# A mixer's u and v as one product in seven parts, with the order of its first half changed

## The chip, the core and the metric

The kernel runs on one core of one Trainium2 chip. The metric is the device time of one execution in microseconds (us), the median over several runs. A profile of one execution gives what each engine did: PE (matmuls), DVE, ACT and POOL (elementwise work), and SP, which like POOL issues transfers.

## The reference

A trunk of two layers over 512 tokens of 1024 channels, in float32. Each layer is a gated feed-forward block, a mixer, and a second feed-forward block; the change is in the mixer.

```python
def rms_norm(x, g):
    y = xf * lax.rsqrt(jnp.mean(xf * xf, axis=-1, keepdims=True) + RMS_EPS)
    return y * g

def mixer(h, w_in, gate_bias, rpb, w_na_out, w_f_out, w_o):    # h = rms_norm(x, gain)
    z = h @ w_in
    q, k, v, uf = four slices of z, 512 columns each;  ga, gf = the rest, 1024 columns each
    y_na = neighbourhood_attention(q, k, v, rpb) @ w_na_out    # 8 heads of 64 channels
    y_f = fourier_mix(uf) @ w_f_out     # real 2-D DFT over positions and 128 channels, 4 groups
    g_na = jax.nn.sigmoid(ga + gate_bias[0])
    g_f = jax.nn.sigmoid(gf + gate_bias[1])
    return (g_na * y_na + g_f * y_f) @ w_o

for l in range(2):
    x = x + 0.5 * swiglu(rms_norm(x, ..), ..)
    x = x + mixer(rms_norm(x, ..), ..)
    x = x + 0.5 * swiglu(rms_norm(x, ..), ..)
return rms_norm(x, final_norm)
```

## The kernel before

Every float32 operand is kept as two parts of a reduced type: a high part, made on ACT (`xh`, `whi`), and the rest, made on DVE (`xl`, `wlo`). A product of two operands is three matmuls, high x high, high x low and low x high (`mm3`, L286 to L288). A 128x512 result fills one of the eight PSUM banks.

**Weights.** `Stream` (object `ws`) walks one list of weight granules of 128x1024, written out by `stage_items` in the order of use. It loads each by a DMA into a `raw` buffer some `FETCH` granules ahead; `prep` then makes `whi` (L175) and `wlo` (L178) from it, with three buffers of each. Sums of weight blocks are made by a second, accumulating DMA on POOL's queue (L146, L180) or on DVE (L160).

**Products in seven parts.** The feed-forward blocks and the mixer's gate and output projections multiply in seven products in place of eight (Strassen's scheme on 2x2 blocks): `strassen` lists the weight blocks a to d and their sums in an order given by product numbers 1 to 7; `product` (L447, L448, L450) runs the 24 matmuls of one product; `snap` (L517) copies an intermediate sum from PSUM, and `less` (L522) subtracts one from PSUM. The mixer's u and v are not made so: `proj_U` makes u, and again u with the token order mirrored, `proj_V` makes v, 96 matmuls of 128x512 each, straight from `xh` and `xl`.

**The norm.** An object made by the stage before holds the transposed input in quads (two channel halves x two token halves). `quad` transposes a quad on PE and splits it, `squares` sums squares on ACT, `rstd` makes the reciprocal root `r` on DVE by three Newton steps, and `spread` (L438, L440) writes `r` to memory and reads it back as the row `R` on all partitions, two DMAs on POOL's queue. For a mixer, `quad` splits straight from PSUM and keeps no raw copy.

**The mixer's order.** Each engine works in order through one queue; the order is mostly as written, with a scheduler that may move work of DVE and ACT by its own due times, except inside `tc.manual_schedule`, where it is as written. The written order of the first half:

- `proj_U`, `proj_V`, `constants()` (tables, by POOL's queue, L951, L954)
- first Fourier stage, `four_pos` for four groups (L1048 to L1051 on DVE)
- projections q0 and k0 (`proj_T`, 24 matmuls; multiplied by R at L970, then split at L292 to L296)
- second Fourier stage, `four_ch` for four groups. Each takes two banks and is evicted by ACT (`fq`) and DVE (`fy`, L1065 to L1067), then split to `y` (L1071, L1072)
- projection q1, then for hp = 0, 1, 2: `att_next(hp)`, projection k of hp+1, the outs of hp-1, projection q of hp+2; then the last steps with rows of y times `w_f_out` (`f_some`) between

`att_next(hp)` is trans(hp-1), 16 transposes of the probabilities (L1140, split to `p` by L292 and L293), then scores(hp), 24 matmuls (L1104); its softmax runs on DVE (L1118, L1127) and ACT (L1124, L1131). `att_outs(hp)`, outs(hp) below, multiplies `p` with v. From step hp = 1 the code reads:

```python
for hp in range(3):
    att_next(hp)
    bias_for(hp + 1)
    proj_k(hp + 1)
    if hp:
        att_outs(hp - 1)
    if hp < 2:
        proj_q(hp + 2)
f_some(2)
```

## Time and profile before

| | |
|---|---|
| Median of three runs | 1904.96 us (1904.66 to 1905.70) |
| Profiled execution | 1906.04 us, of which the span in the profile is 1904.2 |
| PE busy | 1891.7 us, 99% of the span, 9189 matmuls and transposes |
| DVE busy | 1602.4 us, 84% |
| ACT busy | 1161.6 us, 61% |
| POOL busy | 160.7 us, 8% |
| First layer's mixer begins | 337 us |
| Second layer's mixer begins | 1281 us |

A row of the timeline has the start in us, the length in us, engine, line, operation, tiles, size and count, and in brackets how long the engine was idle before it and what ended that. Matmuls are pipelined: a row is longer than the distance to the next, and that distance, the pitch, is what a matmul costs. A line "PE x <- ACT y: a, n, b" of the waits says that PE waited a us in n times, b at the longest, for ACT.

### The profile page before, as it was taken

The numbers are of one execution on the slowest core, as the hardware profiler recorded it, in microseconds if no ns is written. First come the engines' busy times: TensorE is split into PE (matmuls) and PEld (weight loads), VectorE is DVE, ScalarE is ACT, GpSimd is POOL, SyncE is SP. The second block draws the span as 40 slices with busy tenths as digits, with TensorE's granted clock in tenths as the row PEclk, the third lists the DMA queues.
The fourth block names the chain that finished last, engine by engine and source line by source line (L and its number), as shares of the span: only waits on it lengthen the run. The fifth ranks groups of instructions, "written<-read, shape, count | busy, mean of one in ns | idle before, by whom it ended". The sixth has DMA issues, their size and how long they took to land.

```text
span 1904.2 us, 25091 instructions
## 1 busy us (share of the span) xinstructions
PE 1891.7 (99%) x9189; PEld 1586.8 (83%) x9189; DVE 1602.4 (84%) x2000; ACT 1161.6 (61%) x1676; POOL 160.7 (8%) x198
## 2 busy tenths in 40 slices
PE   9999999999999999999999999999999999999998
PEld 7888888888888888888888888888888888888886
DVE  7877899586889987889997778995769899787899
ACT  6655665468566755566665556663675576555655
POOL 0101010000111010001010100100001101000010
PEclk9999999999999999999999999999999999999999
DMA  8776499323886776649877664992247867766594
GB/s 301 202 207 187 150 249 320 105 84 104 217 218 166 180 195 204 177 152 262 251 185 210 187 180 152 268 339 74 68 130 215 215 170 175 207 177 177 170 275 147
DMA packets 104636, 364.36 MB, mean 191 GB/s; under 512 B 12032, under 2 KB 12160, under 8 KB 104512
## 3 DMA queue, kind: packets, MB, share of 16 engines
q1 hardware_dynamic: 77568, 270.70, 40.1%
q0 software_dynamic: 26800, 92.04, 26.8%
q8 instruction: 72, 1.18, 0.2%
q14 instruction: 52, 0.43, 0.1%
q10 hardware_dynamic: 144, 0.02, 0.0%
HBM read 357.46 MB, written 2.11 MB: 189 GB/s over the span
## 4 chain that ended last, share of the span: by engine, by line
PE 95%; issue 2%; DMA 2%; DVE 1%; ACT 0%; POOL 0%; DVEq 0%; ACTq 0%; POOLq 0%; SPq 0%
PE A L447 9%; PE A L448 9%; PE A L450 9%; PE o L448 7%; PE o L447 7%; PE o L450 7%; PE ps L286 5%; PE ps L288 5%; PE ps L287 5%; PE B L448 4%; PE B L447 4%; PE B L450 4%; PE C L448 2%; PE C L447 2%; PE C L450 2%; PE tr L540 2%
## 5 line engine op out<-in xcount | busy, mean ns | idle before, releaser
L175 ACT ACTIVATE whi<-raw 128x1024 fp32r<-128x1024 f32 (+1 forms) x528 | 546.1, 1037 | 423.4 <-PE A L448 123.2
L178 DVE TENSOR_TENSOR wlo<-raw,whi 128x1024 fp32r<-128x1024 f32 (+1 forms) x528 | 627.3, 1193 | 191.2 <-ACT whi L175 186.5
L146 POOL DMA_DIRECT2D raw<-in_wst_dram x158 | 136.2, 873 | 1440.2 <-DMA raw<-in_wst_dram 674.7
L160 DVE TENSOR_TENSOR raw<-raw,raw 128x1024 f32<-128x1024 f32 (+1 forms) x146 | 172.6, 1191 | 1.2
L448 PE MATMUL A<-whi,xl 128*128 128x512 f32 x384 | 149.5, 389 | 0.0
L447 PE MATMUL A<-whi,xh 128*128 128x512 f32 x384 | 149.4, 389 | 0.0
L450 PE MATMUL A<-wlo,xh 128*128 128x512 f32 x384 | 110.5, 389 | 0.0
L170 ACT ACTIVATE whi<-raw 128x1024 fp32r<-128x1024 f32 (+1 forms) x79 | 81.6, 1036 | 40.2 <-PE A L448 12.4
L171 DVE SCALAR_TENSOR_TENSOR wlo<-raw,whi 128x1024 fp32r<-128x1024 f32 (+1 forms) x79 | 93.1, 1193 | 12.2 <-ACT whi L170 12.2
L633 ACT ACTIVATE th<-sn,rh 128x512 f32<-128x512 f32 x80 | 56.8, 714 | 69.4 <-DVE sn L522 69.4
L517 ACT ACTIVATE sn<-A 128x512 f32<-128x512 f32 x96 | 56.4, 589 | 51.3 <-PE A L450 51.2
L450 PEld LDWEIGHTS A<-wlo,xh 128*128 128x128 f32 x384 | 72.1, 188 | 15.0
L448 PEld LDWEIGHTS A<-whi,xl 128*128 128x128 f32 x384 | 72.1, 188 | 14.8
L447 PEld LDWEIGHTS A<-whi,xh 128*128 128x128 f32 x384 | 72.1, 188 | 14.8
L447 PE MATMUL B<-whi,t1h 128*128 128x512 f32 x192 | 76.2, 397 | 0.0
L447 PE MATMUL A<-whi,t3h 128*128 128x512 f32 x192 | 75.3, 392 | 0.4 <-ACT sn L517 0.4
L447 PE MATMUL C<-whi,xh 128*128 128x512 f32 x192 | 74.9, 390 | 0.0
L447 PE MATMUL A<-whi,t2h 128*128 128x512 f32 x192 | 74.9, 390 | 0.0
L448 PE MATMUL B<-whi,t1l 128*128 128x512 f32 x192 | 74.8, 390 | 0.0
L448 PE MATMUL A<-whi,t3l 128*128 128x512 f32 x192 | 74.8, 390 | 0.0
L448 PE MATMUL C<-whi,xl 128*128 128x512 f32 x192 | 74.7, 389 | 0.0
L448 PE MATMUL A<-whi,t2l 128*128 128x512 f32 x192 | 74.7, 389 | 0.0
(409 smaller groups left out, 4748.2 us busy)
## 6 DMA issues: line engine op xcount, KB each, us to landing
raw<-in_wst_dram SPq DMA_DIRECT2D x466, 512.0 KB, 5.4
raw<-in_wst_dram POOLq DMA_DIRECT2D x162, 512.0 KB, 7.9
raw<-in_wst_dram SPq DMA_DIRECT2D x30, 256.0 KB, 3.9
bm<-in_bias_dram SPq DMA_DIRECT2D x16, 384.0 KB, 6.0
vs<-v SPq DMA_DIRECT2D x12, 256.0 KB, 4.9
x<-in_xin_dram SPq DMA_DIRECT2D x4, 512.0 KB, 10.2
raw<-in_wst_dram POOLq DMA_DIRECT2D x8, 256.0 KB, 8.7
dft<-in_dft_dram POOLq DMA_DIRECT2D x8, 256.0 KB, 6.2
```

The costliest lines, as they stand in the source:

```text
L146: G.dma_start(out=self.t, in_=wst[GRAN_AT[self.plus]][:, 0 : self.n], accum_op=ALU.add)
L160: V.tensor_tensor(self.raw.t, self.raw.t, self.add.t, ALU.add)
L170: S.activation(hi, t, AF.Copy, scale=-1.0)
L171: self.last = V.scalar_tensor_tensor(lo, t, -1.0, hi.bitcast(F32), ALU.mult, ALU.subtract)
L175: S.activation(hi[:, cs], t[:, cs], AF.Copy)
L178: self.last = V.tensor_tensor(lo[:, cs], t[:, cs], hi[:, cs].bitcast(F32), ALU.subtract)
L286: PE.matmul(ps, lh, rh, start=start, stop=False, skip_group_check=again)
L287: PE.matmul(ps, lh, rl, start=False, stop=False, skip_group_check=again)
L288: PE.matmul(ps, ll, rh, start=False, stop=stop, skip_group_check=again)
L447: PE.matmul(ps, lh, rh, start=start, stop=False, skip_group_check=again)
L448: PE.matmul(ps, ll, rh, start=False, stop=False, skip_group_check=again)
L450: PE.matmul(ps, lh, rl, start=False, stop=stop, skip_group_check=again)
```

## The change

u and v become one product [u | v] in seven parts (`proj_UV`), in the order 1, 5, 6, 2, 3, 7, 4. u is complete behind the sixth (number 7); its mirrored form is then made from u itself by four matmuls with the mirror matrix. q0, k0, q1 and k1 stand between the products, and the order of DVE and ACT in `proj_UV` is written by hand. The sums of activations need raw quads, so `quad` keeps them for the mixer also; `rstd_steps` takes a square root on ACT and one Newton step; a table load for it stands at the head of the out-projection before a mixer, and one for Exp in the mixer's head. Weight granules of u and v go from 8 to 14 a layer, with loads 8 ahead. The tables are fetched behind product 7, `R` behind product 1.

Behind it the order is: `four_pos`, q2, scores(0), k2, q3, `four_ch`, trans(0), scores(1), outs(0), k3, one row of f, trans(1), scores(2), two rows of f, outs(1), one row of f; from trans(2) on as before, but that two rows of f no longer stand between trans(3) and outs(3). The matmuls' order is the same in both layers. In the diff below the removed bodies of `proj_U`, `proj_V` and `wide` are left out.

```diff
-        def strassen(s, name, idx, sizes, order, dma=False):
+        def strassen(s, name, idx, sizes, order, dma=False, behind=None):
...
+                for key in (behind or {}).get(m, ()):
+                    add(Raw(key))
...
-            for name, n in (("u", 4), ("v", 4), ("qk", 8), ("f", 4)):
-                for g in range(n):
-                    add(Raw((s, name, g)))
+            qk = [(s, "qk", g) for g in range(8)]
+            strassen(s, lambda q: "u" + q, 0, two, (1, 5, 6, 2, 3, 7, 4), True, behind={5: qk[0:1], 6: qk[1:2], 2: qk[2:3], 7: qk[3:4]})
+            for key in qk[4:] + [(s, "f", g) for g in range(4)]:
+                add(Raw(key))
...
-                self.fetch(self.prepped + FETCH)
+                self.fetch(self.prepped + self.depth)
...
         def quad(self, i, j):
+            self.quad_high(i, j)()
+        def quad_high(self, i, j):
...
-            if not self.mix:
-                raw = self.raw[i, j] = slot(F32, "xr")
+            raw = self.raw[i, j] = slot(F32, "xr")
...
+                    S.activation(raw[:, kt, :], tr[:, k, :], AF.Copy, scale=self.gain(4 * i + kt))
+            S.activation(hq, raw, AF.Copy)
+            return lambda: V.tensor_tensor(lq, raw, hq.bitcast(F32), ALU.subtract)
...
-            if self.mix:
-                pc = bank()
-                PE.matmul(pc[:, 0:2], mirror, self.r[:, 3:1:-1], start=True, stop=True)
-                self.rflip = small("rflip", 2)
-                V.tensor_copy(self.rflip, pc[:, 0:2])
-                return
...
+        def rstd_steps(self):
+            ms, q, t = small("ms", 4), small("sq", 4), small("rt", 4)
+            r = self.r = small("r", 4)
+            V.tensor_tensor(ms, self.ssq[:, 0:4], self.ssq[:, 4:8], ALU.add)
+            V.tensor_scalar(ms, ms, 1.0 / D, EPS, ALU.mult, ALU.add)
+            S.activation(q, ms, AF.Sqrt)
+            yield
+            V.reciprocal(r, q)
+            V.tensor_tensor(t, r, r, ALU.mult)
+            V.scalar_tensor_tensor(t, t, -0.5, ms, ALU.mult, ALU.mult)
+            V.scalar_tensor_tensor(r, t, 1.5, r, ALU.add, ALU.mult)
+            yield
+        def flip(self):
+            pc = bank()
+            PE.matmul(pc[:, 0:2], mirror, self.r[:, 3:1:-1], start=True, stop=True)
+            self.rflip = small("rflip", 2)
+            V.tensor_copy(self.rflip, pc[:, 0:2])
...
+    def combos(norm, t4):
+        norm.tiles(0)
+        norm.tiles(1)
+        raw, hx, lx = norm.raw, norm.h, norm.l
+        acts = {1: (hx[0], lx[0], 0), 2: (hx[1], lx[1], 0), 3: (hx[1], lx[1], 256)}
+        if t4:
+            acts[4] = (*t4, 0)
+        def combine(m):
+            p, a, b, op = {
+                5: ((0, 0), (0, 0), (0, 1), ALU.subtract),
+                7: ((0, 1), (0, 1), (1, 1), ALU.subtract),
+                6: ((0, 0), (1, 1), (0, 0), ALU.add),
+                4: ((1, 0), (1, 0), (0, 0), ALU.subtract),
+            }[m]
+            V.tensor_tensor(raw[p], raw[a], raw[b], op)
+            yield
+            if m != 4 or not t4:
+                acts[m] = (slot(F32R, f"t{m}h"), slot(F32R, f"t{m}l"), 0)
+            h, l, _ = acts[m]
+            S.activation(h, raw[p], AF.Copy)
+            yield
+            V.tensor_tensor(l, raw[p], h.bitcast(F32), ALU.subtract)
+            yield
+        return acts, combine
...
-        if late:
+        if late or nxt.mix:
             tc.keep_in_program_order(S.activation(small("sq", 1), ones, AF.Sqrt))
         ps = {}
         for i, (m, c, _) in enumerate(steps):
...
+                    if nxt.mix:
+                        nxt.low01 = nxt.quad_high(0, 1)
+                    else:
+                        nxt.quad(0, 1)
             make(i + 2)
...
+                if not nxt.mix:
+                    nxt.squares(1, 0)
                 nxt.later((1, 0))
...
         def proj_T(scale):
             ps = bank()
             wh, wl = ws.next()
             for kt in range(DT):
                 c = slice(kt * P, (kt + 1) * P)
                 mm3(ps, wh[:, c], wl[:, c], *xs[kt], kt == 0, kt == DT - 1)
+            def out():
+                t = tmp(s="q")
+                V.tensor_tensor(t, ps, R, ALU.mult)
+                hi, lo = hilo("q")
+                if scale is None:
+                    S.activation(hi, t, AF.Copy)
+                else:
+                    S.activation(hi, t, AF.Copy, scale=scale)
+                def rest():
+                    if scale is None:
+                        V.tensor_tensor(lo, t, hi.bitcast(F32), ALU.subtract)
+                    else:
+                        V.scalar_tensor_tensor(lo, t, scale, hi.bitcast(F32), ALU.mult, ALU.subtract)
+                    return hi, lo
+                return rest
+            return out
+        def proj_UV():
+            acts, combine = combos(norm, None)
+            ws.depth = 8
+            with tc.manual_schedule(engines={mybir.EngineType.DVE, mybir.EngineType.Activation}):
+                steps = {m: combine(m) for m in (5, 6, 7, 4)}
+                def step(m, n=1):
+                    for _ in range(n):
+                        next(steps[m])
+                step(5)
+                def t1():
+                    step(5, 2)
+                    norm.squares(1, 0)
+                pa = pair("A")
+                product(pa, acts[1], K4, True, hook=t1)
+                root = norm.rstd_steps()
+                next(root)
+                ws.items[ws.prepped + 1].summed()
+                next(root)
+                norm.spread(R)
+                ws.prep(ws.pos + 3)
+                low10 = norm.quad_high(*norm.due.pop(0))
+                s1 = snap(pa)
+                norm.low01()
+                step(6, 2)
+                pb = pair("B")
+                product(pb, acts[5], K4, True, hook=low10)
+                sb = snap(pb)
+                S.activation(small("sq", 1), ones, AF.Exp)
+                step(6)
+                q0 = proj_T(DH**-0.5)
+                step(7, 2)
+                product(pa, acts[6], K4, False, again=True, hook=lambda: step(7))
+                s2 = snap(pa)
+                k0 = proj_T(None)
+                step(4, 2)
+                q0 = q0()
+                step(4)
+                pc = pair("C")
+                product(pc, acts[2], K4, True)
+                q[0] = q0()
+                q1 = proj_T(DH**-0.5)
+                k0 = k0()
+                less(pc, s1)
+                k[0] = k0()
+                product(pb, acts[3], K4, False, again=True)
+                q1 = q1()
+                less(pb, s2)
+                uh, ul = slot(F32R, "uh", (2, T)), slot(F32R, "ul", (2, T))
+                S.activation(uh, s2, AF.Copy)
+                q[1] = q1()
+                norm.flip()
+                product(pa, acts[7], K4, False, again=True, hook=lambda: V.tensor_tensor(ul, s2, uh.bitcast(F32), ALU.subtract))
+                constants()
+                S.activation(mir, mirror, AF.Copy)
+                flipped = []
                 for c in range(2):
+                    pm = bank()
+                    PE.matmul(pm, mir, uh[:, 1 - c, :], start=True, stop=False)
+                    PE.matmul(pm, mir, ul[:, 1 - c, :], start=False, stop=True)
+                    t = tmp(s="uf")
+                    S.activation(t, pm, AF.Copy, scale=norm.rflip[:, c : c + 1])
+                    flipped.append(t)
+                less(pa, sb)
+                k1 = proj_T(None)
+                us, rest = [[], []], []
                 for c in range(2):
+                    for op in (ALU.add, ALU.subtract):
+                        w = tmp(s="ue")
+                        V.scalar_tensor_tensor(w, s1[:, c, :], norm.r[:, c : c + 1], flipped[c], ALU.mult, op)
+                        hi, lo = hilo("u")
+                        S.activation(hi, w, AF.Copy)
+                        us[c].append((hi, lo))
+                        rest.append((lo, w, hi))
+                        if len(rest) > 1:
+                            l_, w_, h_ = rest.pop(0)
+                            V.tensor_tensor(l_, w_, h_.bitcast(F32), ALU.subtract)
+                vt = [None] * 4
+                def v_out(c, src):
+                    t = vt[c] = slot(F32R, "v", (2, T))
+                    split(t[:, 0, :], t[:, 1, :], src, norm.r[:, c : c + 1])
+                product(pa, acts[4], K4, False, again=True)
+                l_, w_, h_ = rest.pop(0)
+                V.tensor_tensor(l_, w_, h_.bitcast(F32), ALU.subtract)
+                k1 = k1()
+                v_out(2, sb[:, 0, :])
+                k[1] = k1()
+                v_out(3, sb[:, 1, :])
+            ws.depth = FETCH
+            for b in range(2):
+                v_out(b, pa[b])
+            return us, vt
...
         def proj_q(hp):
-            q[hp] = proj_T(DH**-0.5)
+            q[hp] = proj_T(DH**-0.5)()()
         def proj_k(hp):
-            k[hp] = proj_T(None)
-            o.append(hilo("o"))
+            k[hp] = proj_T(None)()()
...
         def att_outs(hp):
+            o.append(hilo("o"))
             for i in (2 * hp, 2 * hp + 1):
                 att_out(i, pt_.pop(i))
...
-        u = proj_U()
-        vt = proj_V()
+        u, vt = proj_UV()
+        def f_rows():
+            for i in range(2):
+                yield from fill(yf, fs, i)
+        f_fill = f_rows()
+        def f_some(n):
+            for _ in range(n):
+                next(f_fill)
+        for g in range(4):
+            four_pos(g)
+        proj_q(2)
         bias_for(0)
         vs = []
         for s in range(3):
...
-        proj_k(0)
+        att_next(0)
+        bias_for(1)
+        proj_k(2)
+        proj_q(3)
         for g in range(4):
             four_ch(g)
-        proj_q(1)
-        def f_rows():
-            for i in range(2):
-                yield from fill(yf, fs, i)
-        f_fill = f_rows()
-        def f_some(n):
-            for _ in range(n):
-                next(f_fill)
-        for hp in range(3):
-            att_next(hp)
-            bias_for(hp + 1)
-            proj_k(hp + 1)
-            if hp:
-                att_outs(hp - 1)
-            if hp < 2:
-                proj_q(hp + 2)
+        att_next(1)
+        bias_for(2)
+        att_outs(0)
+        proj_k(3)
+        f_some(1)
+        att_next(2)
+        bias_for(3)
         f_some(2)
+        att_outs(1)
+        f_some(1)
         B = {(i, j): [z[i].bitcast(F32)[:, :, j * 256 : (j + 1) * 256] for z in (hx, lx)] for i in range(2) for j in range(2)}
         next(first)
         att_next(4)
         swap_pools(0)
-        f_some(2)
         next(first)
...
-        for name, m in (("u", u), ("v", v)):
-            for i in range(4):
-                wst[GRAN_AT[s, name, i]] = _wide(m, (2 * i, 2 * i + 1), 0)
...
         wo = g["mix_w_o"][l]
+        four("u", 0, u, 0, v, 0)
```

More of the change, by code (lines that the diff above doesn't have):

```diff
@@ L67, in _granules @@
                 s = (l, 0)
-                for name, n in (("u", 4), ("v", 4), ("qk", 8), ("f", 4)):
+                for q in "abcd":
+                    for g in range(2):
+                        put(s, "u" + q, 0, g)
+                for name, n in (("qk", 8), ("f", 4)):
                     for g in range(n):
@@ L253, in __init__ @@
             self.stage = 0
+            self.depth = FETCH
         def fetch(self, to):
@@ L551, in stage_ffn @@
         first = norm.idx == 0
-        norm.tiles(1)
         t4 = (hx[0][:, :, 256:512], lx[0][:, :, 256:512])
@@ L567, in plain @@
             late_low(parts)
-        acts = {1: (hx[0], lx[0], 0), 2: (hx[1], lx[1], 0), 3: (hx[1], lx[1], 256), 4: (*t4, 0)}
+        acts, steps_of = combos(norm, t4)
         def combine(m):
-            if m == 5:
-                V.tensor_tensor(raw[0, 0], raw[0, 0], raw[0, 1], ALU.subtract)
-                acts[5] = parts(raw[0, 0], "t1")
-            elif m == 7:
-                V.tensor_tensor(raw[0, 1], raw[0, 1], raw[1, 1], ALU.subtract)
-                acts[7] = parts(raw[0, 1], "t3")
-            elif m == 6:
-                V.tensor_tensor(raw[0, 0], raw[1, 1], raw[0, 0], ALU.add)
-                acts[6] = parts(raw[0, 0], "t2")
-            else:
-                V.tensor_tensor(raw[1, 0], raw[1, 0], raw[0, 0], ALU.subtract)
-                split(*t4, raw[1, 0])
+            for _ in steps_of(m):
+                pass
         if first:
@@ L899, in stage_ffn @@
                 update(ps[7], 1, 0, 1)
-                nxt.squares(1, 0)
+                if not nxt.mix:
+                    nxt.squares(1, 0)
                 nxt.later((1, 0))
@@ L932, in stage_mixer @@
         mp = mix_pool[0]
+        mir = mp.tile([P, P], F32R, tag="mir", name=nm("mir"), bufs=1)
         def tmp(dt=F32, s="x"):
@@ L954, in constants @@
                 tc.keep_in_program_order(G.dma_start(out=rots[hl], in_=src))
-        def wide():
-            wh, wl = ws.next()
-            for k in range(2):
-                c = slice(k * T, (k + 1) * T)
-                yield wh[:, c], wl[:, c]
         def proj_T(scale):
@@ L1020, in proj_V @@
-        def proj_V():
-            pss = [bank() for _ in range(4)]
-            for g in range(4):
-                for k, (wh, wl) in enumerate(wide()):
-                    kt = 2 * g + k
-                    for c in range(4):
-                        lh, ll = [z[:, c * P : (c + 1) * P] for z in xs[kt]]
-                        mm3(pss[c], lh, ll, wh, wl, kt == 0, kt == DT - 1)
-            outs = []
-            for c in range(4):
-                t = slot(F32R, "v", (2, T))
-                split(t[:, 0, :], t[:, 1, :], pss[c], norm.r[:, c : c + 1])
-                outs.append(t)
-            return outs
+            def out():
[13 more added lines that the diff above has]
+                return rest
```

60 lines of the change are left out of this document (3 added, 57 removed).

## The prediction

> **What bounds the kernel now.** I began with the page: the busy shares, then the chain that ended last. Then came the waits of PE, a table by stretches of the span, and the timelines of PE, DVE, ACT and POOL in the first mixer, which begins at 337 us (T below).
>
> ```profile
> PE 1891.7 (99%) x9189; PEld 1586.8 (83%) x9189; DVE 1602.4 (84%) x2000; ACT 1161.6 (61%) x1676; POOL 160.7 (8%) x198
> ...
> PE 95%; issue 2%; DMA 2%; DVE 1%; ACT 0%; POOL 0%; DVEq 0%; ACTq 0%; POOLq 0%; SPq 0%
> ```
> ```profile
> PE ps L132 <- ACT warm L129: 2.7, 1, 2.7
> PE A L447 <- ACT sn L517: 0.4, 2, 0.2
> ```
> ```profile
> 337.00:387.40 50.40, 50.40 (x251) 42.81 (x250) 27.92 (x56) 20.94 (x34) 4.55 (x8) 1.00 0.31 92
> 387.40:408.40 21.00, 21.00 (x123) 17.74 (x121) 18.66 (x43) 10.36 (x17) 0.00 (x0) 1.00 0.32 96
> 408.40:431.30 22.90, 22.90 (x139) 19.69 (x138) 16.00 (x53) 18.10 (x53) 0.00 (x0) 1.00 0.21 68
> ...
> 1281.00:1331.50 50.50, 50.50 (x252) 42.87 (x251) 28.02 (x57) 21.08 (x34) 4.55 (x8) 1.00 0.31 97
> ```
>
> PE is busy 99% of the span and carries 95% of the last chain. It waits 2.7 us for another engine at the start and 0.4 us in all the rest. In the table (length, then busy time of PE, PEld, DVE, ACT and POOL, then granted clock) PE fills every stretch: u, v and the first Fourier stage from 337.0 to 387.4; q0, k0, second Fourier stage, q1 and scores(0) to 408.4; the first attention step to 431.3. The last row is the second layer's head, the same within 0.1 us. So two rules hold: a matmul less is worth its full pitch, and any new wait of PE costs its full length, since nothing gives it back. DVE is only half busy in the head (27.92 of 50.40) but at 18.66 of 21.00 in the Fourier stretch: there the cover is thin.
>
> **The saving.** All durations are of the profiled execution.
>
> ```profile
> 387.42 0.40 PE L286 MATMUL ps<-xh,whi 128*128 128x512 f32 x1
> ...
> 398.33 0.28 PE L286 MATMUL ps<-b,ch 128*128 128x258 f32 x1
> ...
> 401.20 0.40 PE L286 MATMUL ps<-xh,whi 128*128 128x512 f32 x1
> ```
>
> Between the first two rows lie q0 and k0, 48 matmuls of 128x512: 10.91 us, a pitch of 0.227 us; a projection of 24 takes 5.45. The old u and v are 8 weight tiles x 4 banks x 3 = 96 matmuls each, 192. The new form has 7 products of 24 and 4 mirror matmuls, 172. The difference is 20 x 0.227 = 4.54 us a layer, 9.08 in both. No other form of matmul changes in count.
>
> **The new head.** The seven products need sums of activations and of weights, made on DVE and ACT in an order written by hand. From T to the end of product 4, PE has 172 x 0.227 = 39.0 us, four projections = 21.8 and some 0.9 of transposes: 61.7 us.
>
> ```profile
> 398.53 0.69 DVE L970 TENSOR_TENSOR q<-ps,R 128x512 f32<-128x512 f32 x1 [1.53 <-PE ps L288]
> 399.17 0.06 DVE L1062 MEMSET fq<- 128x1 f32 x1
> 399.39 1.23 DVE L178 TENSOR_TENSOR wlo<-raw,whi 128x1024 fp32r<-128x1024 f32 x1 [0.17 <-ACT whi L175]
> 400.54 0.69 DVE L293 TENSOR_TENSOR q<-q,q 128x512 fp32r<-128x512 f32 x1
> 401.14 0.42 DVE L1065 TENSOR_TENSOR fy<-ps,fq 128x256 f32<-128x256 f32 x1
> 401.47 0.15 DVE L1066 COPY fy<-ps 128x1 f32<-128x1 f32 x1
> 401.54 0.41 DVE L1067 TENSOR_TENSOR fy<-ps,fq 128x255 f32<-128x255 f32 x1
> 401.90 0.06 DVE L1062 MEMSET fq<- 128x1 f32 x1
> ...
> 405.94 0.68 DVE L1072 TENSOR_TENSOR y<-fy,y 128x512 fp32r<-128x512 f32 x1
> ```
>
> A 128x1024 operation on DVE holds it 1.15 us (399.39 to 400.54), a 128x512 one 0.60 (400.54 to 401.14). In those 61.7 us the DVE order has 31 of the first kind (18 wlo, 2 weight sums, 8 for the four activation sums and their low halves, 2 low quads, ul) and 22 of the second, with about 1.5 of small ones: 35.7 + 13.2 + 1.5 = 50.4 us. That fits by 11 us on average, but in order, with three whi and three wlo buffers, so that ACT's next whi waits for PE to release one, and what stands behind it on ACT waits too. Placed in order, most steps are there in time; the low half for product 6 is ready only some 0.3 us ahead. The weight of k0 comes behind an Exp table load and the seventh sum on ACT and is some 0.3 to 0.6 late, the mirror's low half 0.1 to 0.2. I take 0.8 us a layer; the bounds are 0 (every slack holds) and 1.5 (each thin place slips by one half-size operation, 0.60, more). The early transposes and moved squares stand in PE's or ACT's free time; an ACT square root in place of three Newton steps shortens r but adds table loads.
>
> ```profile
> 1.17 1.28 ACT L129 ACT_TABLE_LOAD   x1 [1.17 <-PEq L1639]
> ```
> ```profile
> 343.16 0.79 POOL L438 DMA_DIRECT2D row<-r  x1 [26.62 <-DVE r L309]
> 351.96 0.54 POOL L440 DMA_DIRECT2D R<-row  x1 [8.01 <-DMA row<-r]
> ```
> ```profile
> raw<-in_wst_dram POOLq DMA_DIRECT2D x162, 512.0 KB, 7.9
> ```
>
> A load costs 1.28 us on ACT. The one for the square root stands ahead of an out-projection, where ACT's order has room, so I put it at nothing; the Exp one is in the 0.8. R takes two trips on POOL's queue, 8.8 us to the second issue, and at most about as long again to land. It now starts behind product 1, near T+8, lands by T+26, and q0's multiply stands at T+28 in DVE's order. Behind R's wait on that queue stand an accumulating weight load for a later product (issued about T+18, 7.9 to land, its whi wanted at T+30) and later the tables. Those wait for slots until about T+49, land by T+57, and are needed at T+62. Each has 2 us or more; one that failed would cost its lateness, at most a landing time of 7.9. So nothing for DMA.
>
> **The second Fourier stage and attention.** Here I expect the loss. The old order was four_ch (398.33), projection q1 (401.20), scores(0); then trans(0) and scores(1) with projection k2 before outs(0):
>
> ```profile
> 419.39 1.91 PE L1140 MATMUL ps<-ident,s 128*128 128x128 f32 x16
> 421.23 1.69 PE L1104 MATMUL ps<-q,q 64*128 64x256 f32 x24
> ...
> 428.42 0.28 PE L286 MATMUL ps<-p,v 128*128 128x256 f32 x1
> ```
> ```profile
> 410.15 0.42 DVE L1118 CUSTOM_DVE_ANT_0 s<-ps,bm 128x256 f32<-128x256 f32 x1
> ...
> 422.10 2.48 DVE L293 TENSOR_TENSOR p<-ps,p 128x512 fp32r<-128x512 f32 x4
> ```
>
> The four evictions of four_ch took DVE from 398.53 to 406.6, and q1 covered them. The four p lo (422.10) are needed by outs(0) at 428.42; k2 covered them. In the new order scores(0), k2 and q3 stand ahead of four_ch, and four_ch, trans(0), scores(1) and outs(0) follow each other with no projection between. PE's own work from four_ch to the second matmul of outs(0) is 2.87 + 1.84 + 1.65 + 0.12 = 6.5 us. In that time DVE must do, in its built order: q3's multiply, k2 lo, q3 lo, four y lo and the first p lo (8 x 0.60 = 4.8), two wlo (2.3), four fy groups (401.14 to 401.90, 0.76 each, 3.04), four memsets (0.24) and two score rows (0.8): 11.2 us, beginning 0.2 behind four_ch as at 398.53. PE gets its first p lo 11.4 us behind the start of four_ch and stands 4.9 us. That is the lower bound, as q3's multiply can't start before q3 ends and DVE takes its queue in order. It comes in pieces: banks for trans(0) and scores(1) are those of four_ch, then the p lo. In the old trace the same mixture (6.8 us of work from 398.53 to 405.94) took 7.4, so hand-overs add 0.6. ACT adds more:
>
> ```profile
> 410.33 0.51 ACT L1124 ACTIVATE s<-s,nmx 128x256 f32<-128x256 f32 x1 [2.04 <-DVE nmx L1118]
> ...
> 417.49 0.62 ACT L292 ACTIVATE q<-q 128x512 fp32r<-128x512 f32 x1
> ```
>
> Softmax(0) holds ACT 7.2 us and began 3.6 behind its scores (406.76 in the old trace, where its matmuls took the same 1.7 us), so it ends about as q3 does; k2's and q3's high halves, two whi and fq stand behind it. I add 0.4 for that, and up to 2.0 as the upper bound, the longest wait between these two engines in the rows (2.04 at 410.33). Taken: 4.9 + 0.6 + 0.4 = 5.9, between 4.9 and 7.5. Later steps have a projection or f rows between; at outs(3), where two f rows are taken away, 0 to 0.5, taken at 0.
>
> **Sum.** Per layer -4.54 + 0.8 + 5.9 = +2.2, both layers +4.3: the profiled execution goes from 1906.04 (1904.2 span and 1.8 around it) to 1910.4. It lay 1.1 above the median of the runs, 1904.96, so the median goes to 1909.3. The forecast's own range by the bounds is 2 x 0.4 (-4.54 + 0 + 4.9) to 2 x 4.5 (-4.54 + 1.5 + 7.5) more: 1905.8 to 1914.0.
>
> **The rivals.** (1) Faster: the stall at the second Fourier stage doesn't form, and the matmuls are saved in full. The condition is that DVE has q3, k2 and the first fy groups away before trans(0) wants its banks. For it: the 16.00 of 22.90 us that DVE is busy in the first attention step. Against it: the built order and the 18.66 of 21.00. Then -4.54 + 0.8 a layer, 1897.5. It decides where the stall falls under 1.8 us a layer, the point of 0.2% faster.
> (2) The head becomes bound by the coupling of DVE and ACT over the three weight buffers: every product's weights come one operation (1.15) late at three of the later products. That is some 2.7 more a layer beyond the 0.8: 1914.7. For it: 50.4 of 61.7 us in strict order; against it: most slacks are over 1 us.
> (3) The clock of PE falls in the stall and stays down for a while.
>
> ```profile
> 2.73 4.02 PE L132 MATMUL ps<-warm 128*128 128x512 bf16 x9 [2.73 <-ACT warm L129]
> ```
>
> At the start, behind 2.7 us without work, nine matmuls took 4.02 us, 0.45 each against 0.227 later, though the rows show a granted clock of 1.00. Once a layer this costs 9 x 0.22 = 2.0 us, 1913.3. It needs a gap as long as the one at the start, and the stall reckoned above is split between the banks and the p lo, in pieces of about 2 us. The Trainium skill, "TensorE: Matmul & The Clock Gate", section "HAM oscillation", says this of gaps over about 3.4 us between bursts, after which PE runs at half rate. The first row agrees in the rate; no row here shows a gap in the middle of work.
>
> **How the numbers follow.** A difference of 0.2%, 3.8 us, is about what a measurement of this kernel can tell: faster is under 1901.1, slower over 1908.8. Forecast 0.62, of which 0.26 lies within 0.2% and 0.36 above; rival (1) 0.18, faster; rival (2) 0.14 and rival (3) 0.06, slower. That PE's order is other than said has no chance, as it is in the built instructions. So faster 0.18, same 0.26, slower 0.56. The range goes from 1899, which leaves out about two thirds of rival (1), to 1916, which leaves out the upper part of rival (2).
>
> **What would show it.** In the changed profile: 40 fewer 128x512 matmuls; waits of PE of about 12 us over both mixers at the transposes, scores and outs(0) behind four_ch, released by DVE; waits of 0.3 to 0.6 at k0 and at the mirror; none on R or the tables. I am wrong if PE waits under 2 us a layer behind four_ch, or over 3 us a layer in the products, or if matmuls behind a gap come at 0.45.

## The result, and the profile after

| | before | after |
|---|---|---|
| Median | 1905.33 us (1904.66 to 1907.13, 4 runs) | 1916.12 us (1913.34 to 1917.28, 4 runs) |
| Ratio to before | 1 | 1.0053, 95% interval 1.0036 to 1.0070 |
| Profiled execution | 1906.04 us, clock 0.999 | 1916.78 us, clock 0.995 |

The change is slower by 0.53%, 10.8 us, where 4.3 was forecast. The side was right; the size was more than twice the forecast. The time lies 0.1 us over the upper end of the range, 1916; the kernel before also came out 0.4 us slower than in the forecast. The page of the changed kernel begins:

```profile
PE 1895.6 (99%) x9149; PEld 1586.7 (83%) x9149; DVE 1639.1 (86%) x1992; ACT 1195.1 (62%) x1714; POOL 171.7 (9%) x210
...
PE 89%; DVE 5%; ACT 3%; DMA 1%; issue 1%; DVEq 0%; ACTq 0%
```

There are 40 matmuls fewer, as counted, and yet PE is busy 3.9 us longer: that is the first sign of something other than waits. DVE and ACT have come into the last chain with 8%. The waits of PE on other engines (total, times, longest):

```profile
PE ps L135 <- ACT warm L132: 2.7, 1, 2.7
PE ps L1196 <- DVE fq L1155: 1.8, 2, 0.9
PE ps L1196 <- DVE fy L1160: 1.7, 2, 0.9
PE ps L1232 <- ACT fq L1156: 1.7, 4, 0.6
PE ps L294 <- DVE wlo L181: 0.9, 2, 0.5
PE ps L294 <- DVE p L300: 0.4, 2, 0.3
PE ps L293 <- ACT p L299: 0.2, 1, 0.2
PE C L469 <- ACT whi L178: 0.2, 1, 0.2
```

Scores (L1196) and transposes (L1232) wait for the evictions of the second Fourier stage, outs(0) for p: the place that was foretold, in pieces of 0.9 us at most. The timeline of PE there, first layer:

```profile
423.68 0.28 PE L293 MATMUL ps<-b,ch 128*128 128x258 f32 x1
...
426.75 0.66 PE L1232 MATMUL ps<-ident,s 128*128 128x128 f32 x4
427.96 1.26 PE L1232 MATMUL ps<-ident,s 128*128 128x128 f32 x8 [0.55 <-ACT fq L1156]
429.50 0.65 PE L1232 MATMUL ps<-ident,s 128*128 128x128 f32 x4 [0.28 <-ACT fq L1156]
431.05 2.25 PE L1196 MATMUL ps<-q,q 64*128 64x256 f32 x18 [0.89 <-DVE fq L1155]
434.14 0.97 PE L1196 MATMUL ps<-q,q 64*128 64x256 f32 x6 [0.84 <-DVE fy L1160]
435.29 0.58 PE L293 MATMUL ps<-p,v 128*128 128x256 f32 x1 [0.18 <-ACT p L299]
436.13 0.58 PE L294 MATMUL ps<-p,v 128*128 128x256 f32 x1 [0.26 <-DVE p L300]
...
440.99 0.41 PE L295 MATMUL ps<-p,v 128*128 128x256 f32 x1
441.21 0.63 PE L293 MATMUL ps<-xh,whi 128*128 128x512 f32 x1
```

From the first matmul of four_ch (423.68) to the first of outs(0) (435.29) are 11.61 us, of which PE's own work is 6.36 (2.87 + 1.84 + 1.65): 5.25 us are lost to waits. The brackets there add up to 2.74 only, since a row is longer than the pitch and so covers part of each wait. Then outs(0) takes 5.92 us to 441.21 where it took 2.88 before. Its second matmul begins 0.84 behind the first, behind the end of the first p lo: 0.72 more than the pitch of 0.12. From there the other 23 matmuls take 5.08 us (436.13 to 441.21) where 23 x 0.12 = 2.76 were enough: 2.3 us, and that is the clock. The same place in the table by stretches (the eighth number is the granted clock, behind POOL's count):

```profile
434.00:435.00 1.00, 0.86 (x6) 0.77 (x6) 0.99 (x6) 0.88 (x2) 0.00 (x0) 1.00 0.00 0
435.00:436.00 1.00, 0.70 (x2) 0.29 (x1) 1.00 (x3) 1.00 (x3) 0.00 (x0) 0.57 0.00 0
436.00:437.00 1.00, 0.87 (x4) 0.87 (x5) 1.00 (x3) 1.00 (x4) 0.00 (x0) 0.50 0.00 0
440.00:441.00 1.00, 1.00 (x7) 1.00 (x7) 0.66 (x4) 1.00 (x4) 0.00 (x0) 0.50 0.69 135
441.00:442.00 1.00, 1.00 (x4) 0.87 (x4) 0.51 (x3) 1.00 (x4) 0.00 (x0) 0.52 0.67 258
442.00:443.00 1.00, 1.00 (x6) 0.80 (x5) 0.08 (x1) 1.00 (x5) 0.00 (x0) 1.00 0.67 151
```

The row from 435 (0.57) holds 0.86 us of half clock and the one from 441 (0.52) 0.96; so PE has half its clock for 6.8 us, from about 435.1 to 442.0: a 128x256 matmul comes every 0.21 us in place of 0.12. DVE's part of the story, where the first p lo begins 11.5 us behind q3's multiply:

```profile
423.88 0.69 DVE L1011 TENSOR_TENSOR q<-ps,R 128x512 f32<-128x512 f32 x1 [0.83 <-PE ps L295]
...
435.39 2.48 DVE L300 TENSOR_TENSOR p<-ps,p 128x512 fp32r<-128x512 f32 x4
```

The second layer shows the same waits and the same fall of the clock, at 1384.

### The profile page after: what moved, and what is told of

Its sections match the earlier page's. It is cut to its first block, busy times and chain, and to the rows that moved or that the text cites. A ratio compares the mean times of both kernels' runs of the same rounds, so it can differ in the third digit from the quotient of the medians.

```text
span 1915.0 us, 25094 instructions
## 1 busy us (share of the span) xinstructions
PE 1895.6 (99%) x9149; PEld 1586.7 (83%) x9149; DVE 1639.1 (86%) x1992; ACT 1195.1 (62%) x1714; POOL 171.7 (9%) x210
## 4 chain that ended last, share of the span: by engine, by line
PE 89%; DVE 5%; ACT 3%; DMA 1%; issue 1%; DVEq 0%; ACTq 0%
PE A L469 10%; PE A L470 10%; PE A L472 10%; PE o L470 7%; PE o L469 7%; PE o L472 7%; PE B L469 5%; PE B L470 5%; PE B L472 5%; PE C L469 2%; PE C L470 2%; PE C L472 2%; PE ps L294 2%; PE tr L592 2%; PE ps L295 2%; PE ps L293 2%
## 5 line engine op out<-in xcount | busy, mean ns | idle before, releaser
L178 ACT ACTIVATE whi<-raw 128x1024 fp32r<-128x1024 f32 (+1 forms) x536 | 553.4, 1037 | 386.8 <-PE A L470 126.4
L181 DVE TENSOR_TENSOR wlo<-raw,whi 128x1024 fp32r<-128x1024 f32 (+1 forms) x536 | 635.8, 1194 | 171.3 <-ACT whi L178 169.9
L149 POOL DMA_DIRECT2D raw<-in_wst_dram x166 | 145.6, 891 | 1397.1 <-DMA raw<-in_wst_dram 904.6
L173 ACT ACTIVATE whi<-raw 128x1024 fp32r<-128x1024 f32 (+1 forms) x83 | 85.8, 1037 | 43.8 <-PE o L470 12.8
L469 PE MATMUL C<-whi,xh 128*128 128x512 f32 x208 | 81.3, 391 | 0.3 <-ACT whi L178 0.2
L470 PE MATMUL B<-whi,xl 128*128 128x512 f32 x208 | 81.0, 389 | 0.0
L469 PE MATMUL B<-whi,xh 128*128 128x512 f32 x208 | 80.9, 389 | 0.0
L472 PE MATMUL C<-wlo,xh 128*128 128x512 f32 x208 | 59.8, 389 | 0.0
L472 PE MATMUL B<-wlo,xh 128*128 128x512 f32 x208 | 59.8, 389 | 0.0
L469 PE MATMUL B<-whi,t5h 128*128 128x512 f32 x136 | 54.2, 399 | 0.0
L694 DVE TENSOR_TENSOR at<-at,at 128x1024 f32<-128x1024 f32 (+1 forms) x48 | 53.8, 1130 | 0.0
```

Of the source, the lines that this page charges most:

```text
L149: G.dma_start(out=self.t, in_=wst[GRAN_AT[self.plus]][:, 0 : self.n], accum_op=ALU.add)
L173: S.activation(hi, t, AF.Copy, scale=-1.0)
L178: S.activation(hi[:, cs], t[:, cs], AF.Copy)
L181: self.last = V.tensor_tensor(lo[:, cs], t[:, cs], hi[:, cs].bitcast(F32), ALU.subtract)
L469: PE.matmul(ps, lh, rh, start=start, stop=False, skip_group_check=again)
L470: PE.matmul(ps, ll, rh, start=False, stop=False, skip_group_check=again)
```

## The experiments

Ratios are against the kernel before, timed beside each on the same chip; differences are of medians. The theory (A): PE stands wherever DVE and ACT have work that no matmul lies beside, and the thin stretches bring down PE's clock, which costs again. The first rival (B): the loss comes from the seven-product head.

**The first four: put cover back, or fill the gap**

e1 moves q3, e2 moves k3, e3 both:

```diff
         proj_k(2)
-        proj_q(3)          # e1, e3
         for g in range(4):
             four_ch(g)
+        proj_q(3)          # e1, e3
         att_next(1)
         bias_for(2)
+        proj_k(3)          # e2, e3
         att_outs(0)
-        proj_k(3)          # e2, e3
```

> Projection q3 stands between the second Fourier stage and trans(0), all else as in the changed kernel. Theory A (the loss is one queue of DVE work behind the second Fourier stage, 5.2 us of waits of PE a layer, and a half clock of PE that follows from them, 3.0 us a layer): the 5.45 us of q3 cover most of the queue, waits of PE there fall to 0.5 to 1.5 us a layer, the clock stays at 1.00, and the time falls by 12 to 16 us from 1916 to 1900 to 1904. Theory B (the loss sits in the seven-product head and its effects, and the second stage only shows it): the time stays within 3 us of 1916.

> Projection k3 stands between scores(1) and outs(0), all else as in the changed kernel. Theory A with a clock that follows the share of time PE works in over some microseconds: the waits for banks at trans(0) and scores(1) stay (about 4.5 us a layer), only the wait of 0.4 us for p goes, the clock still falls, now over k3, and the time stays at 1913 to 1917. Rival (the clock falls for the last wait, at outs(0), alone): clock at 1.00 throughout, time 6 us lower, about 1909.

> Both moves: q3 between the second Fourier stage and trans(0), k3 between scores(1) and outs(0). Theory A: no wait over 0.5 us a layer in this stretch and the clock at 1.00; what is left against the kernel before is the saving of 4.54 a layer less 0.5 in the head and 0.6 at outs(3): 1905 - 2 x 3.4 = 1898. Theory B: 1913 or more.

Measured: e1 1917.49 us (ratio 1.0066, 1.0051 to 1.0081), e2 1916.13 (1.0059, 1.0044 to 1.0074), e3 1916.17 (1.0062, 1.0045 to 1.0078). e2 came as expected: the waits at the transposes and scores stay, and the clock falls over k3 in place of outs(0) (0.62 on average from 432 to 441 us). e1 and e3 were misses by 13 to 18 us: no faster than the changed kernel. The timeline of e3, PE and then ACT:

```profile
425.00 0.79 PE L293 MATMUL ps<-xh,whi 128*128 128x512 f32 x1 [2.95 <-ACT fq L1156]
```
```profile
422.47 1.69 ACT L1223 ACTIVATE s<-s,rs 128x256 f32<-128x256 f32 x4
424.06 0.61 ACT L1014 ACTIVATE q<-q 128x512 fp32r<-128x512 f32 x1
424.58 0.36 ACT L1156 ACTIVATE fq<-ps 128x255 f32<-128x255 f32 x1
```

q3 itself now waits, 2.95 us. It needs a PSUM bank, the second Fourier stage has written all eight, and the first to come free is held until fq has read it; fq stands on ACT behind the last copies of softmax(0) and a high half of a projection. In the old order softmax(0) came later than that stage; here it comes first. So a projection is no cover by itself: it has to find a bank. And behind that one gap the clock fell as well (0.75 on average over the next 6 us).

e4 leaves all of DVE and ACT as they are, and only gives PE something to do in the gaps:

```diff
+        def idle(ps):
+            for _ in range(3):
+                PE.matmul(ps, hx[0][:, 0, 0:P], hx[0][:, 0, :], start=True, stop=True)
...
             ps = [bank(), bank()]
+            if hp == 1:
+                for p_ in ps:
+                    idle(p_)
...
                 pt = bank()
+                if busy:           # trans(0)
+                    idle(pt)
```

> The changed kernel with 24 more matmuls of 128x512 a layer whose results are overwritten: three ahead of the transposes in each of the four banks of trans(0), three ahead of the scores in each of the four banks of scores(1), 5.4 us of PE work in the place where PE waits. Nothing that DVE does is altered. Theory A, clock by the share of working time: the clock stays at 1.00 behind the stage, saving 3.0 us a layer, while the added work lies mostly in waits that are there anyway (1 to 2 us a layer beyond them): 1911 to 1914. Rival (the clock falls for another reason than idle time, or the waits alone make the loss): the clock falls as before and the time is 1917 to 1922.

Measured: 1912.52 us (1.0038, 1.0023 to 1.0053). With 48 matmuls more than the changed kernel the median is 3.6 us less. The intervals of the two ratios (1.0036 to 1.0070 for the change) overlap at their ends, so the traces have to show where the gain comes from. The stretch in the table, and PE's first matmuls of four_ch and of k3 behind outs(0):

```profile
425.00:441.00 16.00, 15.98 (x116) 13.57 (x115) 15.03 (x46) 11.80 (x29) 0.00 (x0) 1.00 0.00 1
```
```profile
424.86 0.28 PE L293 MATMUL ps<-b,ch 128*128 128x258 f32 x1
...
440.50 0.40 PE L293 MATMUL ps<-xh,whi 128*128 128x512 f32 x1
```

PE is busy throughout and its clock is 1.00. The stretch takes 15.64 us against 17.53 in the changed kernel, 1.9 us a layer, about the 3.6 us of both. outs(0) begins 12.65 us behind four_ch in place of 11.61 and then takes 2.99 in place of 5.92. That shows that the half clock follows from PE's idling and is no property of these matmuls, and that it cost more than the 1.0 us by which the filling delays outs(0).

**The next four: why the cover failed, and order without the new head**

e5 is e3 with scores(0) ahead of q2, so that softmax(0) should be over in time. e6 adds two small moves to it. e7 is e3 with q3 between the second and third group of four_ch. e8 is the kernel before with the new order:

```diff
-        proj_q(2)
...
         att_next(0)
         bias_for(1)
+        proj_q(2)          # e5, e6
         proj_k(2)
...
-                S.activation(small("sq", 1), ones, AF.Exp)       # e6: from behind product 5
+                S.activation(small("sq", 1), ones, AF.Exp)       # e6: to ahead of product 4
...
+        f_some(1)          # e6
         att_outs(3)
-        f_some(1)          # e6
...
-        for g in range(4):
+        for g in range(2):             # e7
             four_ch(g)
         proj_q(3)
+        for g in range(2, 4):          # e7
+            four_ch(g)
```

```diff
         proj_q(0)
         proj_k(0)          # e8, on the kernel before
+        att_next(0)
+        bias_for(1)
+        proj_q(1)
+        proj_k(1)
         for g in range(4):
             four_ch(g)
-        proj_q(1)
...
-        for hp in range(3):
-            att_next(hp)
-            bias_for(hp + 1)
-            proj_k(hp + 1)
-            if hp:
-                att_outs(hp - 1)
-            if hp < 2:
-                proj_q(hp + 2)
-        f_some(2)
+        att_next(1)
+        bias_for(2)
+        att_outs(0)
+        proj_q(2)
+        proj_k(2)
+        att_next(2)
+        bias_for(3)
+        proj_q(3)
+        att_outs(1)
+        proj_k(3)
...
         att_next(3)
-        f_some(2)
+        f_some(3)
         att_outs(2)
-        f_some(1)
+        f_some(2)
```

> As with both moves, but scores(0) right behind the first Fourier stage, ahead of q2, so that its softmax on ACT (7.2 us) is over when the second Fourier stage comes. Theory A2 (with both moves PE waited 3.0 us for fq, ACT's copy of the first Fourier group, which stood behind softmax(0) on ACT, while the second Fourier stage held all eight banks; the half clock followed from that wait): the wait goes and the clock stays at 1.00, 5.6 us a layer less, 1905; up to 3 us a layer more if scores(0) waits for the banks of the first Fourier stage. Rival (the wait is of the eight banks and DVE's queue alone): time as with both moves, 1914 to 1918.

> As the kernel before it (scores(0) early), and two small things: the table load for Exp stands ahead of product 4 in place of behind product 5, and the last row of f stands ahead of outs(3) in place of behind it. Theory A: the 0.5 us a layer of waits at k0 and C, and the 0.4 to 0.8 at outs(3), go: 1.5 to 2 us less than that kernel over both layers, if nothing else comes late. Rival: the late low half of k0's weight is DVE's own queue and the wait stays: within 0.5 us.

> As with both moves (scores(0) behind q2), but q3 stands between the second and the third group of the second Fourier stage, where only four of the eight banks are held. Theory A2: q3 finds a bank at once and covers the wait for softmax(0) on ACT; the 4.1 us of wait and 1.5 of half clock a layer shrink to 1 to 2.5: 1907 to 1912. Rival: the third group waits just as long, 1914 to 1918.

> The kernel before, with its own u and v, but with the order of the change behind them as far as it can be had: q0, k0, scores(0), q1, k1, second Fourier stage, trans(0), scores(1), outs(0), and q2, k2, q3, k3 behind that; no matmul is added or left out. Theory A (order alone makes the loss): waits of 5 us and a half clock of 3 us a layer in the same place, 1905 + 16 = 1921 (1917 to 1924). Theory B (the seven-product head brings it): 1905 to 1908.

Measured: e5 1915.16 us (1.0044, 1.0029 to 1.0059), e6 1918.30 (1.0065, 1.0048 to 1.0082), e7 1916.01 (1.0050, 1.0035 to 1.0065), e8 1923.09 (1.0088, 1.0073 to 1.0103).

e8 came as expected and answers the first question. With no seven-product u and v at all, and no matmul fewer or more, an order of this kind alone adds 17.2 us; theory A gave 16 (12 to 19) and B 3 at most. Its order is not a copy of the change: its waits lie at scores(0), at the second Fourier stage and at p of several steps. But they are waits of the same kind, with a half clock (3.4 us a layer) behind those from the second Fourier stage to outs(0). e5, e6 and e7 missed. e5 failed since the built order of DVE put the score rows of softmax(0) behind all evictions of the first Fourier stage, so that the early scores brought softmax(0) only 0.9 us forward (its first exponential at 415.14 and not 416.06); q3 waited 2.48 us for fq in the same way. In e7 q3 has its bank, and the wait has moved on, to trans(0), scores(1) (1.17 us) and k3:

```profile
427.50 1.09 PE L1232 MATMUL ps<-ident,s 128*128 128x128 f32 x8 [1.45 <-DVE fy L1160]
...
434.36 0.77 PE L293 MATMUL ps<-xh,whi 128*128 128x512 f32 x1 [0.90 <-DVE p L300]
```

e6 is 3.1 us slower than e5 by the medians, though their intervals overlap: the waits at k0 and for p at outs(3) did go, but the first Fourier stage now waits for u (0.31 a layer), and later products for their copies on ACT (1.8 over both layers).

**The last four: less work in the queue, and the old order as far as it reaches**

e9 is e3 with three groups of four_ch, q3, then the fourth, and priority for fq and fy in the built order (not shown below). e10 moves the last row of f ahead of outs(3) as well. e11 takes from e9 the splits of y for groups 2 and 3 (behind k3) and prepares the first weight of f one step later. e12 is the changed kernel with the old order behind the head:

```diff
-        for g in range(4):
+        for g in range(3):             # e9, e10, e11
             four_ch(g)
         proj_q(3)                      # e11: prepares one weight ahead, not two
+        four_ch(3)
         att_next(1)
         bias_for(2)
         proj_k(3)
+        for out in late:               # e11: the splits of y, groups 2 and 3
+            out()
```

```diff
-        att_next(0)
-        bias_for(1)
         proj_k(2)
-        proj_q(3)
         for g in range(4):
             four_ch(g)                 # e12
+        proj_q(3)
+        att_next(0)
+        bias_for(1)
+        proj_k(3)
+        f_some(2)
         att_next(1)
         bias_for(2)
+        f_some(2)
         att_outs(0)
-        proj_k(3)
         f_some(1)
...
         att_next(3)
-        f_some(2)
         att_outs(2)
-        f_some(1)
...
         ws.prep(ws.pos + 2)
-        f_some(1)
```

> As with both moves (scores(0) behind q2), but three groups of the second Fourier stage, q3, and then the fourth, and the evictions of that stage (fq, fy) have priority in the order of ACT and DVE, so that fq of the first group stands between the exponentials of softmax(0) and not behind its last copy. Theory A2 (q3 waits for a bank that fq on ACT holds, behind softmax(0); the half clock follows): no wait over 1 us a layer in this stretch and the clock at 1.00, which is 4.5 to 5.5 us a layer less than with both moves: 1905 to 1907, or down to 1902 if the later steps also keep pace. Rival (cover is short in total, and what is not waited for here is waited for a few steps later): 1912 or more.

> As the kernel before it, with the last row of f ahead of outs(3) in place of behind it. The wait for p at outs(3), 0.8 to 1.1 us a layer with both moves, goes: 1 to 2 us less over both layers. Rival: the same time is waited for at the next products, since the split of the last outputs loses its cover: within 0.5 us.

> As with three groups, q3 and the fourth, and two pieces of work taken out of the queue ahead of the splits of p: the splits of y for groups 2 and 3 (1.2 us on DVE, 1.1 on ACT) stand behind k3, and the first weight of f is prepared one step later (1.15 us on DVE, 1.0 on ACT). Theory A: the 2.6 us a layer of waits in this stretch (for banks and for p) fall under 1, with that the clock stays at 1.00 (3.3 us a layer), and the time falls by 9 to 12 us, to 1904 to 1907. Rival (cover is short in total and the wait only moves again, or the clock falls for smaller waits too): 1912 or more.

> The new head, and behind it the order of the kernel before as far as the four projections and eight rows of f that are left reach: q2, k2, second Fourier stage, q3, scores(0), k3, two rows of f, trans(0), scores(1), two rows, outs(0), one row, trans(1), scores(2), two rows, outs(1), one row; nothing is left to stand behind scores(3) and trans(3). Theory A (PE waits wherever DVE's and ACT's work has no matmuls beside it, and the head has taken four projections of 5.45 us a layer): no wait over 0.5 us and full clock at the second Fourier stage and at trans(0), and in their place waits at outs(2) to outs(3) of 6 to 10 us a layer with a half clock behind them: 1912 to 1922. Rival (the loss is proper to the second Fourier stage behind scores(0)): 1898 to 1903.

Measured: e9 1915.87 us (1.0053, 1.0041 to 1.0065), e10 1916.92 (1.0055, 1.0040 to 1.0070), e11 1910.21 (1.0027, 1.0017 to 1.0036), e12 1921.98 (1.0084, 1.0067 to 1.0101).

In e9 q3 waits no more, and k3 does, for a bank that p holds (1.26 us); with 2.6 us of waits in the stretch the clock still falls. So e9 missed, and its rival (1912 or more) held. e10 missed too: at outs(3) and just behind it PE waits 0.20 us a layer in place of 1.05, but a later product then waits 1.85 us in the first layer and 1.17 in the second for an ACT copy, and behind the 1.85 the clock falls once more, for 3.4 us. In e11 the queue of DVE ahead of p is 2.4 us shorter. Its longest waits of PE, but for the one at the start, and the stretch:

```profile
PE ps L294 <- DVE p L300: 1.7, 2, 0.9
PE ps L1203 <- DVE p L300: 1.3, 2, 0.6
PE ps L294 <- DVE wlo L181: 0.9, 2, 0.5
PE o L472 <- DVE wlo L181: 0.5, 1, 0.5
PE ps L1203 <- ACT fq L1157: 0.4, 2, 0.2
```
```profile
417.00:433.00 16.00, 15.14 (x99) 13.21 (x98) 13.71 (x46) 14.92 (x40) 0.00 (x0) 1.00 0.15 49
433.00:441.00 8.00, 8.00 (x45) 6.86 (x44) 6.90 (x26) 5.60 (x21) 0.00 (x0) 1.00 0.37 107
```

By the list under 1 us a layer of waits is left there (the two rows of L1203), the clock is 1.00, and the time is 5.9 us under the changed kernel. That is 5.7 under e9, where 9 to 12 were expected, and still over the kernel before. Two things lie beside that reading. From the first matmul of scores(1) to k3 are 3.69 us (429.56 to 433.25) where the scores' own work is 1.65, so the stretch still loses 2.0 us a layer; and outs(3) now waits 0.86 us a layer for p (the row of L294 and p), far behind this stretch. The runs of e11 spread from 1908.25 to 1915.98 us at the same recorded clock of 0.998 to 0.999; why, no trace here shows. e12 came as expected: the stretch is clean and the bill comes at the end:

```profile
PE ps L294 <- DVE wlo L181: 6.1, 2, 3.2
PE ps L1232 <- ACT s L1223: 4.5, 4, 1.9
```
```profile
412.00:440.00 28.00, 28.00 (x176) 23.80 (x176) 23.34 (x63) 20.13 (x47) 0.00 (x0) 1.00 0.10 33
440.00:465.00 25.00, 25.00 (x158) 21.86 (x158) 13.07 (x54) 22.42 (x66) 0.00 (x0) 1.00 0.23 74
465.00:480.00 15.00, 11.95 (x90) 9.67 (x89) 9.36 (x30) 12.78 (x36) 0.87 (x1) 0.92 0.38 126
480.00:500.00 20.00, 17.06 (x70) 14.32 (x69) 16.44 (x21) 7.92 (x13) 2.58 (x3) 0.80 1.00 285
```

PE works without a gap to 465 us, then waits at trans(3) for the softmax on ACT and at the product behind outs(3) for a weight, with the clock down to 0.80 on average over the last row. In all the orders tried, where the matmuls stand decided where PE waits; none was free of waits, and none beats the kernel before.

## Why the prediction was right or wrong

Per layer, in the profiled execution of the first:

| Term | predicted | measured |
|---|---|---|
| 20 matmuls fewer | -4.54 | -4.54 (40 fewer on PE's count) |
| Waits in the head | +0.8 (0 to 1.5) | +0.5, at k0 and the first matmuls of product 2 |
| Waits from four_ch to outs(0) | +5.9 (4.9 to 7.5) | +6.0 (5.25 ahead of outs(0), 0.72 in it) |
| Half clock | 0, a rival at 2.0 | +2.7 (2.3 in outs(0), 0.4 in k3) |
| Tail | 0 (0 to 0.5 at outs(3)) | +0.6 |
| Sum | +2.2 | +5.3 |

Twice the measured sum is 10.6 us; the profiled execution grew by 10.7. The range held, or nearly so, by luck: its upper end was drawn for rival (2), a bound head, which did not come, while the forecast's own bounds ended at 1914.0 and had nothing for the clock.

- **The saving and the queue were right.** The list of DVE work behind the second Fourier stage, written from the built order and the old durations, gave the first p lo 11.4 us behind four_ch's first matmul as the bound and 12.4 with the hand-overs and ACT; it ended some 12.3 behind (it began at 435.39, four lasted 2.48), and the matmul that needs it came 12.45 behind. The loss up to there was forecast at 5.9 and measured at 6.0. ACT's fq released some of these waits where the text named DVE alone, and at the mirror there was no wait. Rival (1), that the stall doesn't form, is refuted; rival (2), a bound head, too, since all head waits together are 0.5 us. R and the tables came in time.
- **The clock was the step that failed.** The text left it out of the sum, priced rival (3) at 2.0 us a layer and gave it 0.06, for the reason that it "needs a gap as long as the one at the start". It didn't: the longest wait here is 0.9 us. The sign that the text named for this, matmuls behind a gap at double pitch, came (0.21 for 0.12). e4 shows that the clock doesn't fall where PE has no idle time. Twice its 2.7 us is 5.4 of the 6.8 us between the forecast and the result; most of the rest is the tail. Its price was low too: nine matmuls at the start were taken for the length of the slow time, and it lasted 6.8 us.
- **The sum of the tail was small but not nothing.** With two rows of f taken from ahead of outs(3), PE loses 0.36 us there for p (two matmuls start 0.48 apart for a pitch of 0.12) and waits 0.45 at the product behind it for a wlo, where the old kernel had one wait of 0.20 somewhat later:

```profile
480.75 0.36 PE L293 MATMUL ps<-p,v 128*128 128x256 f32 x1
481.23 0.39 PE L294 MATMUL ps<-p,v 128*128 128x256 f32 x1
...
488.35 0.50 PE L294 MATMUL ps<-wlo,o 128*128 128x512 f32 x1 [0.45 <-DVE wlo L181]
```

- **What the prediction didn't say:** that the lost cover would be missed in every other place too. No move of what is left bought it all back in e1, e3, e5, e7, e9 and e12; e11, the best, got back 5.9 of the 10.8 us. The head took four projections, 21.8 us of PE work a layer, and used them to hide its own sums, and they were missing behind it. Whether the head could do with fewer was not tried.

## What to carry to other kernels

When a change saves matmuls on a busy TensorE by adding work elsewhere, count the matmuls that are left to lie beside each stretch of vector work, bank by bank and in the built order, and not the matmuls saved: here 4.5 us saved a layer cost 6.0 in waits and 2.7 in clock. Several short waits close together were dearer than their sum, as the clock halved behind them; filling them with matmuls that nobody needs was worth 3.6 us. A moved block covers a wait only if it finds a free PSUM bank when it gets there: q3 didn't in e3 and e5, nor k3 in e7 and e9. And add up waits from start to start, against the pitch: the list of waits shows less.

## What the runs showed of the hardware that I had not expected

PE's clock fell to half in the middle of work without one long gap. In the changed kernel the waits ahead of it were 0.55, 0.28, 0.89, 0.84 and 0.18 us within 8 us; in e9 2.6 us of waits with 1.3 as the longest were enough, in e3 one of 2.95; in e11 pieces of 0.22 and 0.64 us were not, nor in e4, where PE's busy share was full. It came back after 6.8 us in the changed kernel. There is a pattern in it. In all the traces a slow stretch inside the program lasted 3.4 us (e3, e6 and e8, both layers) or 6.8 (the changed kernel, e2, e5, e7 and e9, both layers), and the changes of the clock lie whole multiples of 3.413 us apart: the falls of the changed kernel at 435.14 and 1384.04, for one, 278 times that. So the clock looks as if it were set anew every 3.4 us; then the moment at which a wait falls would matter as well as its length, which no run here tried. How much idle time is enough stays open: in the 3.4 us ahead of the fall at 435.14 PE's rows cover 2.55, and in the 3.4 before those 2.24, without a fall between. The Trainium skill, "TensorE: Matmul & The Clock Gate", section "HAM oscillation", which the prediction leaned on, speaks of gaps over about 3.4 us; that is longer than any here, and the measurement decides. The same page's section "A second HAM failure mode: psum-queue depth-cycling" says that frequent small idle times between groups of matmuls, while PSUM banks are cycled, make the clock go up and down. This case agrees, with 0.50 granted for 6.8 us behind five waits of under 0.9.
